# Three ordinary tiles instead of two ahead of the seven-product units, with the units' right factors prepared under the third

## The chip, the core and the metric

The kernel runs on one core of a Trainium2 chip. The metric is the device time of one execution in microseconds (us), as the median of several runs. The engines of the core are named PE (TensorE, matrix products), DVE (VectorE, elementwise), ACT (ScalarE, activations and casts), POOL (GpSimd) and SP (SyncE, which here only issues DMAs). Each of them takes its own instructions in order and waits on semaphores for the others.

## The reference

One layer of a residual block in float32, for 1024 positions of 1024 features:

```
def swiglu(h, w_gate, w_up, w_down):
    return (jax.nn.silu(h @ w_gate) * (h @ w_up)) @ w_down
...
x = x + 0.5 * swiglu(rmsnorm(x, ffn1_norm[l]), ffn1_w_gate[l], ffn1_w_up[l], ffn1_w_down[l])
x = x + hybrid_mixer(rmsnorm(x, mix_norm[l]), w_in[l], conv_w[l], conv_b[l], ...)
x = x + 0.5 * swiglu(rmsnorm(x, ffn2_norm[l]), ffn2_w_gate[l], ffn2_w_up[l], ffn2_w_down[l])
...
return rmsnorm(x, final_norm)
```

The two feed-forward parts (FFN1, FFN2) have 2816 hidden features, which is 22 tiles of 128. The mixer between them is a stick-breaking attention and a short convolution. The change touches only the first half of each feed-forward part, `silu(h @ w_gate) * (h @ w_up)`.

## The kernel before

Every float32 operand of a matrix product is split into a high and a low part: ACT casts the high part (`nc.scalar.copy`, line 169), DVE subtracts it from the operand (line 170). A product is then three matmuls (high by high, high by low, low by high). Activations lie with features on the 128 partitions and positions along the free axis, in two halves of 512 positions (`hf`). So `x` has 8 feature tiles by 2 halves.

`gate_up(i, act, started, nstd)` computes the 22 hidden tiles `m` of feed-forward part `i`. It does the first `nstd` of them (the table `STD`, line 433, gives 2 for each part) as **ordinary tiles**: for gate and then for up, 8 feature tiles by 2 halves by 3 matmuls, so 48 matmuls each and 96 for a tile. They need no normalised activations: `act` holds the split of `x` times the gain, and the factor 1/rms comes in later, on the products. `gated` (lines 449 to 451) scales the gate's product, takes its silu and scales it again; `hidden` (line 683) multiplies by the up product; `Aside.take` (line 649) forms sums and stores them to `c_sp` for the second half.

The remaining hidden tiles are **units**: gate and up weights of one tile are taken as a 2 by 2 block matrix and multiplied with the activations, also a 2 by 2 block matrix, by seven block products instead of eight (P1, P2, P7, P5, P6, Q4, P3). A product has 4 feature tiles of 3 matmuls, so a unit has 84 matmuls, and delivers the gate and the up of a tile. For this the activations must be combined and normalised, once for each part:

- `normed_in_place` (line 700) multiplies a tile of `x` by its gain and by 1/rms, 16 times;
- the generator `right` makes the right factors in the order P1, P2, P7, P5, P6, Q4, P3, 4 tiles each, as sums of normalised tiles (line 544) and their splits (lines 169 and 170). P1 needs four normalised tiles, P2 four others, P7 the eight of the second half.
- `left` makes the left factors of a unit from its weights, which lie in one buffer `raw`: a split for P2 and P1, three sums (lines 482 to 485), a split for P3 and P6, one for P7 and P5, one for Q4.

The first two units run together, product by product ("u.do(name)" for the one, then for the other), so that there are 24 matmuls for each right factor as it is made; all later units run alone. In FFN1 tile 0 is done during the start of the kernel, together with the transposes of `x`, and the call begins with tile 1.

A list scheduler orders each engine's instructions from the order of the program and its dependences; buffers come from pools (72 of 128 by 512 called `s`, 10 of 128 by 1024 called `w` for split weights, 2 of 128 by 2048 called `raw` for loaded weights, 8 PSUM banks `ps`). SP loads weights when a `raw` buffer is free.

Of the kernel before, what the change touches and what calls it, by code (L numbers as in the profile page):

```python
# [13 lines left out]
ALU = mybir.AluOpType  # L14
# [27 lines left out]
def hybrid_block(ctx: ExitStack, tc: tile.TileContext, t: dict):  # L42
    nc = tc.nc
    NK = D // P
# [9 lines left out]
    def nm(s):  # L54
        uid[0] += 1
        return f"{s}_{uid[0]}"

    def s(dt=F32):

        return sb.tile([P, HALF], dt, name=nm("s"), tag="s", bufs=72)  # L60

    def w4(dt=F32R):

        return sb.tile([P, S], dt, name=nm("w"), tag="w", bufs=10)

    def bank():
        return ps.tile([P, HALF], F32, name=nm("ps"), tag="ps", bufs=8)
# [22 lines left out]
    def mm(out, lhs, rhs, **kw):  # L90
        nc.tensor.matmul(out, lhs, rhs, **kw)  # L91
        clock[0] += 1
        while pending and pending[0][0] <= clock[0]:
            next_event()
# [73 lines left out]
    def split(hi, lo, x):  # L168
        nc.scalar.copy(hi, x)  # L169
        nc.vector.tensor_tensor(out=lo, in0=x, in1=f(hi), op=ALU.subtract)  # L170
        return hi, lo
# [47 lines left out]
    W = Stream()  # L219
# [9 lines left out]
    def wk(w, k):  # L229
        return (w[0][:, k * P : (k + 1) * P], w[1][:, k * P : (k + 1) * P])  # L230

    def both(outs, w, nk, rhs):

        for k in range(nk):
            first, last = k == 0, k == nk - 1
            wh, wl = wk(w, k)
            for hf in range(2):
                rh, rl = rhs(k, hf)
                mm(outs[hf], wh, rh, start=first, stop=False)
                yield  # L240
                mm(outs[hf], wh, rl, start=False, stop=False)
                yield
            for hf in range(2):
                mm(outs[hf], wl, rhs(k, hf)[0], start=False, stop=last)
                yield

    def run(gen):
        for _ in gen:
            pass
# [180 lines left out]


    VORDER = ((2, 6), (3, 7), (0, 4), (1, 5))
    STD = (2, 2)
    N_MIXER = 8 + 8 + 12 + 12

    def all_weights():
        yield from ffn_weights(0, "ffn1", STD[0])
        yield from mixer_weights()
        yield from ffn_weights(1, "ffn2", STD[1])

# [3 lines left out]
    def gated(g, act):  # L444

        o = [s(), s()]
        for hf in range(2):
            rms = act.row(hf)
            nc.vector.tensor_tensor(out=o[hf], in0=rms, in1=g[hf], op=ALU.mult)
            nc.scalar.activation(o[hf], o[hf], AF.Silu)  # L450
            nc.vector.tensor_tensor(out=o[hf], in0=o[hf], in1=rms, op=ALU.mult)
        return o
# [7 lines left out]
    def left(raw, n=HALF, late="P7"):  # L460


        a = {}

        def blk(i, m=1):
            return raw[:, i * n : (i + m) * n]

        def pair(dt=F32R):
            return w4(dt)[:, : 2 * n]

        def halves(hi, lo, *names):
            for i, name in enumerate(names):
                a[name] = (hi[:, i * n : (i + 1) * n], lo[:, i * n : (i + 1) * n])

        def two(ap):
            return ap.rearrange("p (n c) -> p n c", c=n)

        yield a
        halves(*split(pair(), pair(), blk(0, 2)), "P2", "P1")
        yield  # L480
        y = pair(F32)
        nc.vector.tensor_tensor(out=two(y), in0=two(blk(1, 2)), in1=blk(3).unsqueeze(1).to_broadcast([P, 2, n]),  # L482
                                op=ALU.add)
        nc.vector.tensor_tensor(out=blk(3), in0=y[:, :n], in1=blk(2), op=ALU.add)
        nc.vector.tensor_tensor(out=blk(0), in0=blk(3), in1=blk(0), op=ALU.add)
        yield

        def wide():
            hi, lo = pair(), pair()
            split(two(hi), two(lo), two(raw[:, : 4 * n])[:, 0::3])  # L490
            halves(hi, lo, "P3", "P6")

        def narrow():
            halves(*split(pair(), pair(), y), "P7", "P5")

        for step in (wide, narrow) if late == "P7" else (narrow, wide):
            step()
            yield
        a["Q4"] = split(s(F32R)[:, :n], s(F32R)[:, :n], blk(2))
        L.load()  # L500
        yield
# [33 lines left out]
    def right(x, y):  # L535

        b = {}
        yield b

        def parts(name, tiles):  # L540
            b[name] = [split(s(F32R), s(F32R), a) for a in tiles]

        def comb(out, i, j, op):
            nc.vector.tensor_tensor(out=out, in0=i, in1=j, op=op)  # L544
            return out

        def four(k0, hf):
            return [y(k0 + i, hf) for i in range(4)]

        b11 = four(4, 0)  # L550
        parts("P1", b11)
        yield
        b21 = four(0, 0)
        parts("P2", b21)
        yield
        b22, b12, t3 = [], [], []
        for i in range(4):
            b22.append(y(i, 1))
            b12.append(y(4 + i, 1))
            t3.append(comb(s(), b22[i], b12[i], ALU.subtract))  # L560
        parts("P7", t3)
        yield
        t1 = [comb(b11[i], b11[i], b12[i], ALU.subtract) for i in range(4)]
        parts("P5", t1)
        yield
        t2 = [comb(b12[i], t1[i], b22[i], ALU.add) for i in range(4)]
        parts("P6", t2)
        yield
        parts("Q4", [comb(b21[i], t2[i], b21[i], ALU.subtract) for i in range(4)])
        yield  # L570
        parts("P3", b22)
        yield
# [62 lines left out]
    class Aside:  # L635
# [12 lines left out]
        def comb(self, out, x, y, op):  # L648
            nc.vector.tensor_tensor(out=out, in0=x, in1=y, op=op)
            return out  # L650
# [26 lines left out]
    def gate_up(i, act, started, nstd):  # L677

        out = Aside(i)

        def hidden(m, o, u):
            for hf in range(2):
                nc.vector.scalar_tensor_tensor(out=o[hf], in0=o[hf], scalar=0.5, in1=u[hf], op0=ALU.mult,
                                               op1=ALU.mult)
                out.take(m, hf, o[hf])

        for m in range(nstd):
            if m == 0 and started:
                continue
            g, u = [bank(), bank()], [bank(), bank()]  # L690
            run(both(g, W(), NK, act))
            if m == 1 and started:
                hidden(0, gated(started[0], act), started[1])
            o = gated(g, act)
            run(both(u, W(), NK, act))
            hidden(m, o, u)

        def normed_in_place(k, hf):
            x = act.x[k, hf]
            nc.vector.scalar_tensor_tensor(out=x, in0=x, scalar=gain(act.gname, k), in1=act.row(hf),  # L700
                                           op0=ALU.mult, op1=ALU.mult)
            return x

        rights = right(act.x, normed_in_place)
        b = next(rights)
        preps = [left(L.take()[0]) for _ in range(2)]
        units = [Unit(next(p), b, out(nstd + j)) for j, p in enumerate(preps)]
        for p in preps:
            next(p)
        for name in ALL:  # L710
            next(rights)
            for p in preps:
                next(p, None)
            for u in units:
                u.do(name)
        act.x.clear()
        x_tiles.clear()
        prep = left(L.take()[0])
        a = next(prep)
        run(prep)  # L720
        for m in range(nstd + 2, NF):
            unit = Unit(a, b, out(m))
            if m + 1 < NF:
                prep = left(L.take()[0])
                a = next(prep)
            else:
                prep = iter(())
                makers[i] = Prep(i)
                makers[i].begin(0)
            for n, name in enumerate(FEW):  # L730
                unit.do(name)
                next(prep, None)
                if i in makers:
                    makers[i].step()
                    makers[i].upto(UPTO[0] * (n + 1))
            run(prep)
        makers[i].end()
# [234 lines left out]
    g, u = [bank(), bank()], [bank(), bank()]  # L972
# [4 lines left out]
    warm(2, turn(*turns.pop(0)))  # L977
    W.left = 2 * (STD[0] - 1)
    for k in range(NK):
# [14 lines left out]

    gate_up(0, act0, (g, u), STD[0])

# [19 lines left out]
    vt = []  # L1016
    W.left = N_MIXER + 2 * STD[1]
    for hf in range(2):
# [284 lines left out]
    for p in range(4):  # L1303
        for head, hf in ((2 * p, 0), (2 * p, 1), (2 * p + 1, 0), (2 * p + 1, 1)) if p < 3 else (
                (6, 0), (7, 0), (6, 1), (7, 1)):
            prev, y = None, []
            for b in range(4 * hf + 3, -1, -1):
                u, steps = unit(head, hf, b, prev, y)
# [39 lines left out]


    gate_up(1, act2, None, STD[1])  # L1350
    gb = [s(), s()]
    for i in range(2):
# [65 lines left out]
```

## Time and profile before

| | us |
|---|---|
| median of 3 runs | 1920.36 |
| lowest and highest of them | 1918.93, 1923.02 |
| the profiled execution, its own time | 1924.48 |
| its span, from the first to the last instruction | 1922.8 |
| PE busy in the span | 1835.9 (95%) |
| DVE busy | 1393.1 (72%) |
| ACT busy | 897.9 (47%) |

A row of a timeline gives the start, the time to the end of the last instruction, the engine, the line in the kernel, the operation, the tiles written and read, and how many instructions are merged into it; in brackets stands how long the engine was idle before it and which instruction of which engine ended that. Matmul rows go by the name of the helper's line (L91). Matmuls overlap: one of 512 columns has a mean duration of 394 ns in the profile, while back to back they follow each other more closely. A few per cent of the matmul records can be missing, so counts of matmuls are taken from the program.

### The profile page before, as it was taken

How to read it: one execution, taken by the hardware profiler on the slowest of the kernel's cores; microseconds unless marked ns; L12 is line 12 of the kernel's file. 1: busy time of each engine (PE TensorE's matmuls, PEld its weight loads, DVE VectorE, ACT ScalarE, POOL GpSimd, SP SyncE). 2: the span in 40 equal slices, each digit the busy share in tenths (PEclk: the TensorE clock that was granted, in tenths of full speed). 3: DMA queues.
4: the chain of work that ended last, by engine and by line, in shares of the span. 5: the costliest groups of instructions: out<-in, count | busy, mean ns of one | idle time of the engine just before them, and what ended most of it. 6: DMA issues, size and time to landing. Idle time of an engine off the chain costs nothing.

```text
span 1922.8 us, 23200 instructions
## 1 busy us (share of the span) xinstructions
PE 1835.9 (95%) x8176; PEld 1507.5 (78%) x8176; DVE 1393.1 (72%) x2179; ACT 897.9 (47%) x1608; POOL 253.5 (13%) x400
## 2 busy tenths in 40 slices
PE   6889999999999979999999999989999999988997
PEld 5668888888888858888888878867888888767775
DVE  4897667666777787668787898668676666755768
ACT  4543222223555554667677775533322222444544
POOL 1101001110222120110101000100010101021211
PEclk8899999999999999999999999989999999999998
DMA  7114323334999843341313343304333333588985
GB/s 236 65 55 131 110 90 108 112 104 143 239 230 230 229 165 83 80 99 34 94 44 72 100 142 111 106 33 122 105 108 113 101 102 108 169 184 200 207 195 176
DMA packets 252933, 246.93 MB, mean 128 GB/s; under 512 B 14176, under 2 KB 197008, under 8 KB 252816
## 3 DMA queue, kind: packets, MB, share of 16 engines
q1 hardware_dynamic: 217072, 157.87, 27.6%
q0 software_dynamic: 35744, 87.58, 18.0%
q8 instruction: 64, 1.05, 0.2%
q14 instruction: 53, 0.43, 0.1%
HBM read 150.76 MB, written 85.20 MB: 123 GB/s over the span
## 4 chain that ended last, share of the span: by engine, by line
PE 69%; issue 15%; DVE 9%; DMA 3%; POOL 3%; ACT 1%; SPq 1%; POOLq 0%; DVEq 0%; ACTq 0%
PE ps L91 68%; DVE w L170 1%; DVE s L870 1%; POOL r_sp L830 1%; DMA w<-c_sp 1%; POOL c_sp L646 1%; DVE s L170 1%; DMA raw<-in_ffn_w_gate 1%; DVE s L269 1%; DVE s L176 1%; PE ps L277 0%; DVE s L700 0%; DMA s<-x_sp 0%; PE ps L1087 0%; DVE s L544 0%
## 5 line engine op out<-in xcount | busy, mean ns | idle before, releaser
L91 PE MATMUL ps<-s,w 128*128 128x512 f32 x6352 | 1525.2, 394 | 61.7 <-ACT s L175 13.6
L91 PEld LDWEIGHTS ps<-s,w 128*128 128x128 f32 x6352 | 1192.3, 190 | 320.0 <-DVE s L170 17.4
L169 ACT CAST w<-raw 128x1024 fp32r<-128x1024 f32 (+2 forms) x158 | 157.5, 998 | 278.6 <-PE ps L91 187.9
L170 DVE TENSOR_TENSOR w<-raw,w 128x1024 fp32r<-128x1024 f32 (+2 forms) x158 | 182.0, 1153 | 117.6 <-PE ps L91 60.2
L91 PE MATMUL ps<-s,s 128*128 128x512 f32 (+3 forms) x968 | 249.0, 385 | 7.5 <-ACT s L853 6.5
L91 PEld LDWEIGHTS ps<-s,s 128*128 128x128 f32 x968 | 184.1, 191 | 48.9 <-ACT s L853 8.3
L646 POOL DMA_DIRECT2D c_sp<-s x154 | 83.5, 542 | 777.7 <-DVE s L632 610.9
L170 DVE TENSOR_TENSOR w<-w,w 128x768 fp32r<-128x768 f32 (+2 forms) x104 | 105.8, 1017 | 84.8 <-PE ps L91 44.3
L170 DVE TENSOR_TENSOR s<-s,s 128x512 fp32r<-128x512 f32 (+2 forms) x181 | 119.0, 670 | 43.1 <-ACT s L169 42.7
L169 ACT CAST w<-w 128x768 fp32r<-128x768 f32 (+2 forms) x104 | 91.7, 881 | 92.5 <-DMA w<-c_sp 41.6
L169 ACT CAST s<-s 128x512 fp32r<-128x512 f32 (+2 forms) x181 | 105.0, 607 | 51.6 <-DMA s<-c_sp 30.3
L628 ACT ACTIVATE s<-s 128x512 f32<-128x512 f32 x40 | 25.3, 633 | 201.6 <-DVE s L627 201.5
L170 DVE TENSOR_TENSOR s<-raw,s 128x512 fp32r<-128x512 f32 (+2 forms) x133 | 87.7, 667 | 24.2 <-ACT s L169 23.8
L169 ACT CAST s<-raw 128x512 fp32r<-128x512 f32 (+2 forms) x133 | 77.9, 602 | 36.4 <-DVE raw L766 36.4
L482 DVE TENSOR_TENSOR w<-raw 128x1024 f32<-128x1024 f32 (+2 forms) x56 | 63.1, 1128 | 43.4 <-PE ps L91 43.4
L613 ACT ACTIVATE s<-ps 128x512 f32<-128x512 f32 x40 | 23.8, 598 | 122.8 <-PE ps L91 122.8
L1241 DVE TENSOR_TENSOR s<-s,ps 128x128 f32<-128x128 f32 (+2 forms) x96 | 52.6, 548 | 16.8 <-ACT s L1237 16.4
L1229 ACT ACTIVATE s<-ps 128x128 f32<-128x128 f32 (+2 forms) x96 | 47.0, 490 | 37.7 <-PE ps L91 37.4
L619 DVE TENSOR_TENSOR s<-s,ps 128x512 f32<-128x512 f32 x40 | 27.4, 686 | 47.8 <-PE ps L91 47.8
L830 POOL DMA_DIRECT2D r_sp<-s x48 | 41.6, 876 | 154.7 <-DVE s L855 50.5
L1237 ACT ACTIVATE s<-s 128x128 f32<-128x128 f32 (+2 forms) x96 | 50.2, 523 | 20.6 <-DVE s L1233 19.3
L830 POOL DMA_DIRECT2D x_sp<-s x48 | 41.6, 866 | 125.4 <-DVE s L855 57.7
(133 smaller groups left out, 1697.2 us busy)
## 6 DMA issues: line engine op xcount, KB each, us to landing
c_sp<-s POOLq DMA_DIRECT2D x154, 256.0 KB, 2.5
raw<-in_ffn_w_gate SPq DMA_DIRECT2D x43, 512.0 KB, 3.9
raw<-in_ffn_w_up SPq DMA_DIRECT2D x43, 512.0 KB, 5.2
x_sp<-s POOLq DMA_DIRECT2D x80, 256.0 KB, 4.3
s<-c_sp SPq DMA_DIRECT2D x77, 256.0 KB, 6.5
r_sp<-s POOLq DMA_DIRECT2D x64, 256.0 KB, 5.1
w<-c_sp SPq DMA_DIRECT2D x72, 192.0 KB, 5.0
raw<-in_ffn_w_down SPq DMA_DIRECT2D x11, 1024.0 KB, 8.9
```

What stands on the lines that cost most here:

```text
L91: nc.tensor.matmul(out, lhs, rhs, **kw)
L169: nc.scalar.copy(hi, x)
L170: nc.vector.tensor_tensor(out=lo, in0=x, in1=f(hi), op=ALU.subtract)
L482: nc.vector.tensor_tensor(out=two(y), in0=two(blk(1, 2)), in1=blk(3).unsqueeze(1).to_broadcast([P, 2, n]), op=ALU.add)
L613: last_silu[0] = nc.scalar.activation(self.s0, o, AF.Silu)
L619: nc.vector.tensor_tensor(out=self.u3, in0=self.u2, in1=self.o[2], op=ALU.add)
L628: last_silu[0] = nc.scalar.activation(self.u2, self.u2, AF.Silu)
L646: nc.gpsimd.dma_start(out=self.sp[FACTORS.index(self.names[i]), j], in_=x)
L830: nc.gpsimd.dma_start(out=self.acc(self.g + 4 * i, hf), in_=x, accum_op=ALU.add)
L1229: behind(nc.scalar.activation(u["s"][:, cols], u["z"][:, cols], AF.Exp), table_set)
L1237: nc.scalar.activation(sc, sc, AF.Ln, bias=1.0)
L1241: nc.vector.tensor_tensor(out=sc, in0=sc, in1=u["z"][:, cols], op=ALU.max)
```

## The change

`STD` becomes 3 for both parts. The right factors' generator is started before the loop over ordinary tiles. Under the last ordinary tile it is advanced by one step between the gate's and the up's products (P1's four normalisations and splits) and by two after `hidden` (P2's; then the normalisation of the other eight tiles, for which `right` gets a step of its own). The loop over products skips the steps that were made. Each part so has 3 ordinary tiles and 19 units, of which the pair is tiles 3 and 4.

```
-    STD = (2, 2)
+    STD = (3, 3)
...
-        b22, b12, t3 = [], [], []
-        for i in range(4):
-            b22.append(y(i, 1))
-            b12.append(y(4 + i, 1))
-            t3.append(comb(s(), b22[i], b12[i], ALU.subtract))
+        b22, b12 = four(0, 1), four(4, 1)
+        yield
+        t3 = [comb(s(), b22[i], b12[i], ALU.subtract) for i in range(4)]
         parts("P7", t3)
...
+        rights = right(act.x, normed_in_place)
+        b = next(rights)
         for m in range(nstd):
             if m == 0 and started:
                 continue
+            ahead = m == nstd - 1
             g, u = [bank(), bank()], [bank(), bank()]
             run(both(g, W(), NK, act))
             if m == 1 and started:
                 hidden(0, gated(started[0], act), started[1])
             o = gated(g, act)
+            if ahead:
+                next(rights)
             run(both(u, W(), NK, act))
             hidden(m, o, u)
-
-        def normed_in_place(k, hf):
...
-        rights = right(act.x, normed_in_place)
-        b = next(rights)
+            if ahead:
+                next(rights)
+                next(rights)
+
         preps = [left(L.take()[0]) for _ in range(2)]
...
         for name in ALL:
-            next(rights)
+            if name not in b:
+                next(rights)
```

PE has 8058 instructions before and 8082 after. How the queues read at the places in question follows, for FFN1; FFN2 reads alike. In the changed file line 683 is 681, 700 is 687 and 649 is 647.

The first place is DVE's queue where the ordinary tiles end and the units begin. Before, from `hidden` of tile 1 (L683, which reads the up product `ps`) to the first low parts of P1's right factors (L170, `s<-s,s`) and of the units' weights (L170, `w<-raw,w`); between them stand normalisations (L700) and the sums of `Aside` (L649):

```order
L683 SCALAR_TENSOR_TENSOR s_638<-s_638,ps_501 128x512
L683 SCALAR_TENSOR_TENSOR s_639<-s_639,ps_502 128x512
L700 SCALAR_TENSOR_TENSOR s_195<-s_195,gains_146,s_570 128x512
L649 TENSOR_TENSOR s_698<-s_635,s_639 128x512
L649 TENSOR_TENSOR s_623<-s_639,s_623 128x512
L649 TENSOR_TENSOR s_703<-s_698,s_638 128x512
L700 SCALAR_TENSOR_TENSOR s_215<-s_215,gains_146,s_570 128x512
L170 TENSOR_TENSOR s_719<-s_235,s_718 128x512
L170 TENSOR_TENSOR w_793<-raw_492,w_792 128x1024
L170 TENSOR_TENSOR s_723<-s_253,s_722 128x512
```

After, the same place in the program, P1's low parts and `hidden` of tile 2 (L681); L451 is the last step of `gated` of tile 2, L485 a sum of weights, L544 the sums for P5:

```order
L170 TENSOR_TENSOR s_787<-s_253,s_786 128x512
L485 TENSOR_TENSOR raw_654<-raw_654 128x512
L170 TENSOR_TENSOR s_791<-s_271,s_790 128x512
L485 TENSOR_TENSOR raw_725<-raw_725 128x512
L170 TENSOR_TENSOR s_795<-s_289,s_794 128x512
L170 TENSOR_TENSOR w_927<-raw_654,w_926 128x1024
L544 TENSOR_TENSOR s_235<-s_235,s_378 128x512
L544 TENSOR_TENSOR s_253<-s_253,s_393 128x512
L544 TENSOR_TENSOR s_271<-s_271,s_411 128x512
L544 TENSOR_TENSOR s_289<-s_289,s_426 128x512
L681 SCALAR_TENSOR_TENSOR s_770<-s_770,ps_713 128x512
L681 SCALAR_TENSOR_TENSOR s_771<-s_771,ps_714 128x512
```

All of P1's low parts now stand ahead of `hidden` of the last ordinary tile, where before they stood behind it.

The second place is DVE's queue from P2's right factors to P7's. Before, with P5's sums first (three of L544), then the low part of the first unit's P7 and P5 weights (L170, `w<-w,w`), the four differences for P7 (L544), the same weights of the second unit, and P7's first low part:

```order
L544 TENSOR_TENSOR s_235<-s_235,s_378 128x512
L544 TENSOR_TENSOR s_253<-s_253,s_393 128x512
L544 TENSOR_TENSOR s_271<-s_271,s_411 128x512
L170 TENSOR_TENSOR w_861<-w_734,w_860 128x1024
L544 TENSOR_TENSOR s_830<-s_307,s_378 128x512
L544 TENSOR_TENSOR s_834<-s_325,s_393 128x512
L544 TENSOR_TENSOR s_838<-s_345,s_411 128x512
L544 TENSOR_TENSOR s_842<-s_360,s_426 128x512
L170 TENSOR_TENSOR w_865<-w_738,w_864 128x1024
L170 TENSOR_TENSOR s_845<-s_830,s_844 128x512
```

After, with P2's four low parts first (L170, `s<-s,s`):

```order
L170 TENSOR_TENSOR s_857<-s_159,s_856 128x512
L170 TENSOR_TENSOR s_861<-s_175,s_860 128x512
L170 TENSOR_TENSOR s_865<-s_195,s_864 128x512
L170 TENSOR_TENSOR s_869<-s_215,s_868 128x512
L170 TENSOR_TENSOR w_987<-w_888,w_986 128x1024
L544 TENSOR_TENSOR s_962<-s_307,s_378 128x512
L544 TENSOR_TENSOR s_964<-s_325,s_393 128x512
L544 TENSOR_TENSOR s_966<-s_345,s_411 128x512
L544 TENSOR_TENSOR s_968<-s_360,s_426 128x512
L170 TENSOR_TENSOR w_991<-w_892,w_990 128x1024
L170 TENSOR_TENSOR s_971<-s_962,s_970 128x512
```

P2's low parts have come together ahead of it and no normalisation stands there any more; the order from the first unit's weights over the four differences to P7's first low part is the same.

The third place is PE at the end of P2. Before, the matmuls of the two units (banks `ps_742` and `ps_757`) alternate to the end, and P7 (`ps_868`) begins:

```order
L91 MATMUL ps_757<-s_785,w_710 128x512
L91 MATMUL ps_757<-s_784,w_711 128x512
L91 MATMUL ps_742<-s_789,w_706 128x512
L91 MATMUL ps_742<-s_788,w_707 128x512
L91 MATMUL ps_757<-s_788,w_710 128x512
L91 MATMUL ps_757<-s_789,w_710 128x512
L91 MATMUL ps_757<-s_788,w_711 128x512
L91 MATMUL ps_868<-s_844,w_860 128x512
```

After, the first unit's P2 (`ps_896`) is finished before the second's (`ps_911`) begins, as it stands in FFN2 before the change too:

```order
L91 MATMUL ps_896<-s_868,w_880 128x512
L91 MATMUL ps_896<-s_869,w_880 128x512
L91 MATMUL ps_896<-s_868,w_881 128x512
L91 MATMUL ps_911<-s_856,w_884 128x512
L91 MATMUL ps_911<-s_857,w_884 128x512
L91 MATMUL ps_911<-s_856,w_885 128x512
```

Between the two programs nothing else is in another order on PE, ACT or DVE than these stretches of FFN1 and FFN2; POOL's and SP's queues hold the same kinds of instructions in the same order.

## Rows read from the trace of the kernel before

**Rows 1.** The page: the span, and busy time of the engines.
```profile
span 1922.8 us, 23200 instructions
...
PE 1835.9 (95%) x8176; PEld 1507.5 (78%) x8176; DVE 1393.1 (72%) x2179; ACT 897.9 (47%) x1608; POOL 253.5 (13%) x400
```

**Rows 2.** The page: shares by engine of the chain that ended last.
```profile
PE 69%; issue 15%; DVE 9%; DMA 3%; POOL 3%; ACT 1%; SPq 1%; POOLq 0%; DVEq 0%; ACTq 0%
```

**Rows 3.** Timeline of PE in FFN1, from 60 to 140 us.
```profile
74.01 12.18 PE L91 MATMUL ps<-s,w 128*128 128x512 f32 x53
91.43 6.78 PE L91 MATMUL ps<-s,w 128*128 128x512 f32 x22 [5.24 <-DVE s L170]
99.49 6.06 PE L91 MATMUL ps<-s,w 128*128 128x512 f32 x24 [1.28 <-ACT s L169]
108.27 1.22 PE L91 MATMUL ps<-s,w 128*128 128x512 f32 x2 [2.72 <-ACT s L169]
111.17 20.71 PE L91 MATMUL ps<-s,w 128*128 128x512 f32 x82 [1.67 <-DVE s L170]
131.71 5.60 PE L91 MATMUL ps<-s,s 128*128 128x512 f32 x24
```

**Rows 4.** Timeline of PE in FFN2, from 1232 to 1400 us.
```profile
1233.44 34.65 PE L91 MATMUL ps<-s,w 128*128 128x512 f32 x152
1269.30 0.51 PE L91 MATMUL ps<-s,w 128*128 128x512 f32 x1 [1.20 <-ACT s L169]
1272.78 6.81 PE L91 MATMUL ps<-s,w 128*128 128x512 f32 x23 [2.98 <-DVE s L170]
1280.83 6.00 PE L91 MATMUL ps<-s,w 128*128 128x512 f32 x24 [1.24 <-ACT s L169]
1288.60 0.73 PE L91 MATMUL ps<-s,w 128*128 128x512 f32 x2 [1.76 <-ACT s L169]
1290.66 21.42 PE L91 MATMUL ps<-s,w 128*128 128x512 f32 x82 [1.33 <-DVE s L170]
1311.92 0.39 PE L91 MATMUL ps<-s,s 128*128 128x512 f32 x1
...
1354.57 2.88 PE L91 MATMUL ps<-s,s 128*128 128x512 f32 x12
...
1373.61 2.88 PE L91 MATMUL ps<-s,s 128*128 128x512 f32 x12
```

**Rows 5.** Timeline of DVE, FFN1, as the ordinary tiles end.
```profile
86.37 1.27 DVE L683 SCALAR_TENSOR_TENSOR s<-s,ps 128x512 f32<-128x512 f32 x2
...
88.23 1.88 DVE L649 TENSOR_TENSOR s<-s,s 128x512 f32<-128x512 f32 x3
...
90.03 0.74 DVE L700 SCALAR_TENSOR_TENSOR s<-s,gains,s 128x512 f32<-128x512 f32 x1
90.70 0.68 DVE L170 TENSOR_TENSOR s<-s,s 128x512 fp32r<-128x512 f32 x1
```

**Rows 6.** Busy time of DVE under ordinary tiles: stretch, length, PE, PEld, DVE, ...
```profile
60.00:86.00 26.00, 26.00 (x111) 21.27 (x110) 21.09 (x37) 14.14 (x29) 4.14 (x4) 0.93 0.06 21
1234.00:1268.00 34.00, 34.00 (x151) 27.88 (x149) 23.50 (x35) 6.22 (x9) 1.08 (x2) 1.00 0.05 17
```

**Rows 7.** Timeline of DVE in FFN2 at P7.
```profile
1285.24 1.22 DVE L170 TENSOR_TENSOR w<-w,w 128x1024 fp32r<-128x1024 f32 x1 [1.93 <-ACT w L169]
1286.38 2.49 DVE L544 TENSOR_TENSOR s<-s,s 128x512 f32<-128x512 f32 x4
1288.79 1.22 DVE L170 TENSOR_TENSOR w<-w,w 128x1024 fp32r<-128x1024 f32 x1
```

**Rows 8.** Stretches after P7's waits: length, PE busy, granted clock (1.00 is 2.4 GHz).
```profile
108.00:116.00 8.00, 6.06 (x15) 0.57 0.00 0
1289.00:1297.00 8.00, 6.67 (x19) 0.57 0.00 0
```

**Rows 9.** The page: weight loads, KB each, median us from issue to landing.
```profile
raw<-in_ffn_w_up SPq DMA_DIRECT2D x43, 512.0 KB, 5.2
```

More of the change, by code (lines that the diff above doesn't have):

```diff
@@ L685, in hidden @@
                 out.take(m, hf, o[hf])
[L687 to L696, printed above, removed]
         def normed_in_place(k, hf):
@@ L705, in gate_up @@
         b = next(rights)
+        for m in range(nstd):
+            if m == 0 and started:
+                continue
+            ahead = m == nstd - 1
+            g, u = [bank(), bank()], [bank(), bank()]
+            run(both(g, W(), NK, act))
+            if m == 1 and started:
+                hidden(0, gated(started[0], act), started[1])
+            o = gated(g, act)
+            if ahead:
+                next(rights)
+            run(both(u, W(), NK, act))
+            hidden(m, o, u)
+            if ahead:
+                next(rights)
+                next(rights)
         preps = [left(L.take()[0]) for _ in range(2)]
```

## The prediction

> **What bounds the kernel now.** I read the page first: PE is busy 95% of a span of 1922.8 us, DVE 72% [rows 1], and of the chain that ended last 69% lies on PE, 15% is issue and only 9% is DVE [rows 2]. So PE's own instructions bound the kernel, and what can be had besides is found where PE stands still. The change works at one place in each feed-forward part, so next I read PE's timeline there. What the reader is to see is the bracket at the start of each row. In FFN1 PE waits 5.24 us for a low part before P1, 1.28 us before P2, 2.72 and 1.67 us in P7 [rows 3]; in FFN2 1.20 and 2.98 us, 1.24 us, 1.76 and 1.33 us [rows 4]. Then DVE's timeline at the same place: from 86.37 us it does `hidden` (L683), the sums (L649) and the last normalisation (L700), and only at 90.70 us the first low part of P1 [rows 5]. PE waits for a queue of DVE, not for data that are missing.
>
> **The price of a matmul.** A steady unit has 84 matmuls and comes round from 1354.57 to 1373.61 us [rows 4], so 19.04 us, or 0.2267 us a matmul. As the profile gives one 0.39 us (the single matmul at 1311.92 us [rows 4]), a run of matmuls ends in its row 0.17 us after the next could have started. I take that off wherever a run ends.
>
> **What P1 and P2 lose now.** P1 and P2 of the pair have 24 matmuls each, which should take 5.44 us.
> - FFN1 [rows 3]: tile 1 ends at 74.01 + 12.18 - 0.17 = 86.02. P1 starts at 91.43, a loss of 5.41. It ends at 91.43 + 6.78 - 0.17 = 98.04, after 6.61 us, 1.17 too many. P2 starts at 99.49, 1.45 later, and ends at 105.38, 0.45 too late. Together 8.48 us.
> - FFN2 [rows 4]: tile 1 ends at 1267.92, P1 at 1272.78 + 6.81 - 0.17 = 1279.42. That is 11.50 us for 5.44, a loss of 6.06. P2 starts at 1280.83 (1.41) and ends at 1286.66 (0.39). Together 7.86 us.
>
> These 16.34 us are what the change can remove by its own aim. They include what the clock cost after the first wait, since they are counted by time and not by the brackets.
>
> **What P7 loses now.** From the end of P2 to the first matmul of Q4 there are 84 matmuls (P7, P5, P6 of the pair, P1 of the next unit), 19.04 us. FFN1 takes 131.71 - 105.38 = 26.33, a loss of 7.29 us [rows 3]; FFN2 1311.92 - 1286.66 = 25.26, a loss of 6.22 us [rows 4]. Of the 6.22 us, 3.09 are the two waits. The rest is the clock: over the 8 us after P7 begins its mean is 0.57 [rows 8], so with levels of 0.5 and 1 it was at the lower one for 0.43 / 0.5 x 8 = 6.9 us.
>
> **What is added.** An ordinary tile has 96 matmuls and replaces a unit of 84. Twice 12 matmuls are the 24 by which PE's queue grows: 24 x 0.2267 = +5.44 us. Nothing hides them, since PE is what is waited for. The units' product work on DVE and ACT gets less by a unit in each part; neither is the bound there, so I count nothing for it. Loads stay equal in number and bytes. The third tile's two matrices go into two `raw` buffers in place of one; the next two loads then wait for these to be split. They land 5.2 us after their issue [rows 9], and a tile lasts 96 x 0.2267 = 21.76 us, so this is hidden, by about a tile.
>
> **What is moved, and whether it fits.** DVE has room under the ordinary tiles: it is busy 21.09 of 26 us in FFN1 and 23.50 of 34 us in FFN2 [rows 6], and the third tile gives another 21.76 us. Steps on DVE from the rows: 0.60 us for an operation of 512 columns (three in 1.88 us), 0.67 for a normalisation (90.03 to 90.70) [rows 5], 1.14 for one of 1024 columns (1285.24 to 1286.38) [rows 7].
>
> FFN1, along the changed queue from 86.37 us, where `hidden` of tile 1 can start, to P1's last low part: 3 normalisations (2.0), 4 operations of 1024 columns on the units' weights (4.6), and 17 of 512 columns (2 of `hidden`, 3 of `Aside`, 4 of `gated`, 4 sums of weights, 4 low parts: 10.2). The sum is 16.8 us, so 103.2 us. PE ends tile 2 at 86.02 + 21.76 = 107.78: P1's factors are there 4.6 us early. In FFN2 the queue waits for tile 2's gate product, at 1267.92 + 10.88 = 1278.80, and has about 7.3 us to go from there, so 1286.1 against 1289.68. P1 starts without a wait in both.
>
> P2's low parts stand behind `hidden` of tile 2. From its start these are 2 x 0.60, one of 1.14, one sum of 0.60 and 4 x 0.60, so 5.3 us, while PE spends 5.44 us on P1. As P2 uses its four tiles one after the other, 0.68 us each, the last is needed 2 us later. So both losses go, 16.34 us.
>
> **Where the stall goes: P7 stays.** Its four differences (L544) stand behind the low part of the first unit's P7 weights (L170, `w<-w,w`) in DVE's queue, before and after. DVE is held at that row until ACT has cast these weights (the bracket of 1.93 us) and then does it at 1285.24, the differences at 1286.38, the second unit's weights at 1288.79 [rows 7], and P7's first low part behind them; PE waits for a cast of the differences and then for that low part. The chain starts from the end of the first unit's P2, and the change does not move it ahead of that. So I let P7 lose in both parts what FFN2 loses now, 6.22 us. For FFN1 that is a gain of 7.29 - 6.22 = 1.07 us, since there the two units' P2 now run one after the other as in FFN2, and the first unit's ends a good 2 us sooner.
>
> **The sum.** -16.34 + 5.44 - 1.07 = -11.97 us. The profiled execution took 1924.48 us, 4.12 above the median of 1920.36. 1924.48 - 11.97 = 1912.5, on the scale of the median 1908.4.
>
> **Bounds of the uncertain terms.** What P7 costs is bounded below by its two waits alone (3.09 us) and above by FFN1's 7.29 us: -3.1 to +1.1 us for each part. What remains of P1's and P2's losses is 0 by the queue's count, and at most all of it.
>
> **The rivals.**
> - *The clock is not cut at P7.* For it: before, P7's waits of 1.76 and 1.33 us come some 15 us after a longer stop [rows 4], and the waits of 1.28 and 1.24 us before P2 are followed by matmuls at full rate (24 in 6.06 and 6.00 us). With P1's stop gone, PE comes to P7 from an unbroken run. Against it: P7's own two waits with two matmuls between are unchanged, and the clock fell right behind them in both parts [rows 8]. It saves 3.1 us in each part: 1905.3 or 1902.2 us. The Trainium skill (TensorE: Matmul & The Clock Gate, Part 1) says that the gate follows how busy PE has been of late, and that idling brings the lower rate back. Taken for the whole stretch, that rule gives this rival's time; taken for P7's own waits alone, it gives the forecast. The rows do not decide between the two.
> - *A part of the wait returns.* DVE's count has 4.6 and 3.6 us of slack before P1. But ACT casts the second unit's weights ahead of P1's four tiles, and both engines wait for `w` buffers that PE frees; a wait of 3 us in one or both parts, now before P1 or P2, gives 1911 to 1915 us.
> - *It works in one part only*, for instance because FFN2's queue, which stands at tile 1's `hidden` until 1267.9 us, runs later than counted: 7.9 us come back, 1916.3 us.
> - *Slower: the pair's weights come late.* The second unit's `raw` buffer is now the one that tile 2's up matrix occupies until it is split, where before all four matrices of the pair were asked for long ahead. ACT holds all P1 casts behind the cast of this buffer. P1 then starts when the load lands, and DVE's rows behind it shift along. Against it: the split stands under tile 1, more than 20 us ahead, against 5.2 us for a load [rows 9]. It decides once P1 starts over 6 us after tile 2's end in both parts: then the 12 us are eaten and the time is 1920 or more; with all of P1's and P2's losses still there it is 1920.4 + 5.4 = 1925.8 us. That is also the time if the change does not do what it says.
>
> **How the numbers follow.** Forecast 55%; no cut of the clock in one part or both 22%; a part of the wait 13%; one part only 5%; slower or no change by late weights 5%. The range of 1902 to 1916 us holds the first three. Forecast alone: 1906 to 1911. A difference of 0.2% (3.8 us) is about what a measurement of this kernel can tell from none. The first three lie beyond that, and the one-part case by a hair, so I count half of it as no change: faster 0.90, same 0.06, slower 0.04.
>
> **What would show it.** In the changed profile PE should run without a wait of half a us from 60 us to the end of P2 in FFN1, at 86.02 + 21.76 + 10.88 = 118.7 us. FFN1 gains 8.48 + 1.07 - 2.72 = 6.83 us, so P2 of FFN2 should end at 1267.92 - 6.83 + 32.64 = 1293.7 us, again with nothing before it. Two short waits should follow each, released by ACT L169 and DVE L170, and the clock's mean behind them should be near 0.57 (forecast) or near 1 (first rival). PE has 24 matmuls more. A wait before P1 released by ACT or by a load would show the second or the last rival. The forecast is wrong if the new queue stalls where I counted it as free, above all at `w` buffers, which I counted from the order alone, or if other stretches of the kernel change with no cause in the program's order.

## The result, and the profile after

| | before | after | ratio, 95% interval |
|---|---|---|---|
| medians, us (4 and 4 runs) | 1921.44 | 1905.76 | 0.9912 [0.9894, 0.9930] |
| profiled execution: its time, its span | 1924.48, 1922.8 | 1899.17, 1897.4 | |

The kernel is faster by 15.7 us. The execution that was profiled after is the fastest of its four (the others took 1904.0 to 1909.4), and that of before was above its median, so 25.4 us lie between the two traces. Page of after, which answers to [rows 1]:

```profile
span 1897.4 us, 23215 instructions
PE 1828.5 (96%) x8200; PEld 1504.0 (79%) x8200; DVE 1381.8 (73%) x2167; ACT 892.7 (47%) x1602; POOL 252.8 (13%) x400
```

PE does 24 matmuls more (8200 for 8176) in less busy time. PE's timeline of after, FFN1 [rows 3]; the last row begins Q4 of tile 12:

```profile
72.47 44.39 PE L91 MATMUL ps<-s,w 128*128 128x512 f32 x195
118.40 0.73 PE L91 MATMUL ps<-s,w 128*128 128x512 f32 x2 [1.54 <-ACT s L169]
120.46 20.39 PE L91 MATMUL ps<-s,w 128*128 128x512 f32 x82 [1.33 <-DVE s L170]
140.69 0.39 PE L91 MATMUL ps<-s,s 128*128 128x512 f32 x1
141.68 5.89 PE L91 MATMUL ps<-s,s 128*128 128x512 f32 x23 [0.60 <-DVE s L617]
...
297.25 2.88 PE L91 MATMUL ps<-s,s 128*128 128x512 f32 x12
```

The same of FFN2 [rows 4]; the last row is Q4 of tile 6, which before begins at 1373.61:

```profile
1224.94 67.29 PE L91 MATMUL ps<-s,w 128*128 128x512 f32 x296
1293.83 0.73 PE L91 MATMUL ps<-s,w 128*128 128x512 f32 x2 [1.59 <-ACT s L169]
1295.89 19.03 PE L91 MATMUL ps<-s,w 128*128 128x512 f32 x82 [1.33 <-DVE s L170]
1314.76 0.39 PE L91 MATMUL ps<-s,s 128*128 128x512 f32 x1
...
1357.14 2.88 PE L91 MATMUL ps<-s,s 128*128 128x512 f32 x12
```

The reader is to see the first row of each: 195 and 296 matmuls in one run, to the end of P2, without a bracket. The brackets of 5.24 and 1.28 us [rows 3], 1.20, 2.98 and 1.24 us [rows 4] are gone; P7's two are still there, and FFN1 has a new one of 0.60 us in the pair's Q4. The 195 also tell what the rows of before hold. Up to the end of P2 the change adds the 96 matmuls of one tile, and 195 - 96 = 99 are the 53 + 22 + 24 of [rows 3]. P1 has 24, so its first two stand in the row of 53, ahead of the wait, and 51 are tile 1's.

**How much of it lies at the changed places.** In each part I measure from the first matmul behind the sums of squares (74.01 and 1233.44 before, 72.47 and 1224.94 after) to Q4 of a tile that both programs do as a unit. Tile 12 of FFN1 before, on PE's timeline:

```profile
306.95 2.88 PE L91 MATMUL ps<-s,s 128*128 128x512 f32 x12
```

FFN1 takes 232.94 us before and 224.78 after, FFN2 (to tile 6) 140.17 and 132.20: -8.2 and -8.0, together -16.1 us. That is about the gain of the medians. The other 9 us of the profiles lie behind tile 6 of FFN2 (-8.9 us; 1.5 us less ahead of FFN1 and 1.2 us more between the parts nearly cancel), almost all in the last 270 us, where the programs are alike. The windows over that stretch, to the end of the span (stretch, length, busy time of PE, PEld, DVE, ACT, POOL, the granted clock, and last the DMA's share and GB/s), of before, of after, and of two more executions of the changed kernel (experiments *again* and *again2*):

```profile
1660.00:1930.00 270.00, 230.31 (x947) 183.63 (x946) 180.60 (x293) 121.46 (x222) 51.51 (x61) 0.94 0.77 192
```
```profile
1643.00:1930.00 287.00, 225.18 (x948) 179.32 (x947) 180.96 (x294) 121.91 (x223) 51.39 (x61) 0.97 0.72 180
```
```profile
1647.00:1930.00 283.00, 226.38 (x945) 180.34 (x943) 179.89 (x292) 122.31 (x222) 51.43 (x61) 0.96 0.73 183
```
```profile
1648.00:1930.00 282.00, 231.17 (x948) 182.84 (x947) 181.04 (x294) 122.25 (x223) 51.37 (x61) 0.94 0.74 183
```

The same matmuls keep PE busy for 225.2, 226.4 and 231.2 us in one and the same program, with the clock at a mean of 0.97, 0.96 and 0.94; before, with 230.3 us, lies among them. The windows reach past the end of the span; up to it they are 262.8, 254.4, 257.2 and 262.7 us long. One and the same program takes up to 8 us more here in one execution than in another, so these 9 us are no sign of the change.

### The profile page after: what moved, and what is told of

It reads as the page before. It is cut to its first block, busy times and chain, and to the rows that moved or that the text cites. A ratio compares the mean times of both kernels' runs of the same rounds, so it can differ in the third digit from the quotient of the medians.

```text
span 1897.4 us, 23215 instructions
## 1 busy us (share of the span) xinstructions
PE 1828.5 (96%) x8200; PEld 1504.0 (79%) x8200; DVE 1381.8 (73%) x2167; ACT 892.7 (47%) x1602; POOL 252.8 (13%) x400
## 4 chain that ended last, share of the span: by engine, by line
PE 55%; issue 28%; DVE 7%; POOL 4%; DMA 3%; ACT 1%; SPq 1%; POOLq 0%; DVEq 0%; ACTq 0%
PE ps L91 54%; POOL c_sp L644 2%; DVE s L875 1%; DMA w<-c_sp 1%; POOL r_sp L835 1%; DVE w L170 1%; DVE s L269 1%; DVE s L176 1%; DVE s L170 1%; DMA s<-c_sp 1%; DMA raw<-in_ffn_w_gate 0%; DMA raw<-in_ffn_w_down 0%; ACT w L169 0%; DMA s<-in_x 0%; PE ps L277 0%
## 5 line engine op out<-in xcount | busy, mean ns | idle before, releaser
L91 PE MATMUL ps<-s,w 128*128 128x512 f32 (+1 forms) x6400 | 1523.1, 392 | 40.9 <-DVE s L845 13.3
L170 DVE TENSOR_TENSOR w<-raw,w 128x1024 fp32r<-128x1024 f32 (+2 forms) x158 | 181.8, 1153 | 111.3 <-PE ps L91 55.6
L91 PE MATMUL ps<-s,s 128*128 128x512 f32 (+3 forms) x944 | 242.7, 383 | 8.4 <-ACT s L858 6.0
L91 PEld LDWEIGHTS ps<-s,s 128*128 128x128 f32 x944 | 178.7, 190 | 49.0 <-ACT s L858 7.9
L170 DVE TENSOR_TENSOR w<-w,w 128x768 fp32r<-128x768 f32 (+2 forms) x102 | 103.3, 1013 | 77.8 <-PE ps L91 40.6
L170 DVE TENSOR_TENSOR s<-s,s 128x512 fp32r<-128x512 f32 (+2 forms) x181 | 118.7, 670 | 40.8 <-ACT s L169 40.3
L170 DVE TENSOR_TENSOR s<-raw,s 128x512 fp32r<-128x512 f32 (+2 forms) x131 | 86.2, 666 | 24.0 <-ACT s L169 23.6
L611 ACT ACTIVATE s<-ps 128x512 f32<-128x512 f32 x38 | 22.7, 598 | 113.2 <-PE ps L91 113.2
```

The lines of the kernel that those rows point to most:

```text
L611: last_silu[0] = nc.scalar.activation(self.s0, o, AF.Silu)
```

## The experiments

Each version is timed against the kernel before on its chip, in five rounds. The columns FFN1 and FFN2 give the difference to before of the two stretches just defined, from each version's one trace, matched matmul by matmul (for *four* some units later); the median is that of all runs.

| version | FFN1 | FFN2 | sum | median | ratio, 95% interval |
|---|---|---|---|---|---|
| again | -8.3 | -7.9 | -16.1 | -16.2 | 0.9915 [0.9899, 0.9931] |
| again2 | -8.2 | -5.4 | -13.6 | -14.9 | 0.9916 [0.9896, 0.9936] |
| tile_only | -1.9 | +1.7 | -0.2 | -1.3 | 0.9998 [0.9981, 1.0014] |
| move_only | +1.1 | -10.4 | -9.2 | -8.5 | 0.9959 [0.9945, 0.9973] |
| four | -5.8 | -4.8 | -10.6 | -8.9 | 0.9958 [0.9944, 0.9973] |
| p1_late | -4.2 | -1.9 | -6.1 | -8.1 | 0.9960 [0.9947, 0.9972] |
| p2_late | -7.3 | -5.8 | -13.1 | -14.9 | 0.9930 [0.9911, 0.9949] |
| two_three | +2.5 | -6.7 | -4.2 | -7.1 | 0.9960 [0.9945, 0.9975] |
| three_two | -8.2 | -8.0 | -16.2 | -18.7 | 0.9899 [0.9878, 0.9921] |
| t3early | -7.5 | -5.9 | -13.4 | -13.8 | 0.9918 [0.9894, 0.9942] |
| lead | -12.0 | -10.5 | -22.5 | -19.8 | 0.9896 [0.9878, 0.9915] |
| lead_three_two | -12.0 | -14.0 | -26.0 | -25.2 | 0.9866 [0.9847, 0.9885] |

The theory: P1 and P2 waited for DVE's and ACT's queues, and the gain comes from the factors' low parts standing ahead of the last tile's finish, with a tile to hide under. The main rival: the third tile does it alone, since the scheduler brings normalisations forward by itself.

**again, again2** (the changed kernel). 

> The changed kernel once more, nothing altered. If the gain lies where the trace shows it, the P1 and P2 waits are gone again in both parts, the ratio to before is 0.991 to 0.994 (about -12 to -16 us), and the step from P7 to the next product differs between the two parts only with the granted clock there. If part of the 15.7 us came from a lucky clock in the last stage, the time comes out nearer -12 us and the last stage shows about the cuts of before.

> The changed kernel unaltered, on the chip of the next three, so that they are compared with it directly. Theory: 0.991 to 0.993 of before, as in its two earlier comparisons (0.9912 and 0.9915), with no wait ahead of P1 and P2, and at P7 the same two waits; whether a cut of the granted clock follows them differs from one execution to the next.

Both held: P1 and P2 have no wait in either, and the ratio came out alike three times. They also show how one program differs from execution to execution at P7. In *again2* the second part loses 2.6 us more there, with the same brackets (1.59 and 1.33 us). Windows of the 10 us from P7's start, FFN1 and FFN2, of the first trace of after, then of *again2*:

```profile
118.00:128.00 10.00, 8.28 (x29) 6.41 (x29) 10.00 (x17) 7.21 (x14) 0.00 (x0) 0.83 0.01 2
1294.00:1304.00 10.00, 8.67 (x37) 6.80 (x38) 10.00 (x17) 6.64 (x13) 0.00 (x0) 1.00 0.00 0
```
```profile
121.00:131.00 10.00, 8.17 (x28) 6.36 (x29) 10.00 (x17) 7.31 (x14) 0.00 (x0) 0.83 0.01 2
1296.00:1306.00 10.00, 8.46 (x23) 6.40 (x24) 10.00 (x17) 7.01 (x14) 0.00 (x0) 0.66 0.00 0
```

FFN2's clock there is 1.00 in one and 0.66 in the other; no other difference shows at that place.

**tile_only** (the kernel before with the third tile).

```
-    STD = (2, 2)
+    STD = (3, 3)
```

> The kernel before with three ordinary tiles per part, the factor code left where it was. Theory (the factors' low parts must stand ahead of the last tile's finish on VectorE): that finish still stands in front of P1's factors, so a wait of 3.5 to 4 us stays ahead of P1 in each part and the third tile costs 5.4 us: -2 to -6 us against before, ratio 0.997 to 0.999. Rival 1 (the third tile alone gives the cover, since the normalisations slip under it by themselves): the same as the changed kernel, -12 us or more, ratio 0.991 to 0.993. Rival 2 (a tile without moved code only adds products): +5 us, ratio 1.003.

The main rival fell: without the moved code the gain is gone (0.9998). The theory had the place right and the size too favourable (it said -2 to -6 us). PE's timeline of FFN2:

```profile
1233.79 56.41 PE L91 MATMUL ps<-s,w 128*128 128x512 f32 x248
1291.45 0.73 PE L91 MATMUL ps<-s,w 128*128 128x512 f32 x2 [1.25 <-ACT s L169]
1293.69 8.17 PE L91 MATMUL ps<-s,w 128*128 128x512 f32 x22 [1.50 <-DVE s L170]
1303.06 5.99 PE L91 MATMUL ps<-s,w 128*128 128x512 f32 x24 [1.19 <-ACT s L169]
```

The brackets ahead of P1 and P2 add up to 3.94 us, against 5.42 before [rows 4]. But behind them 22 matmuls take 8.17 us, so P1 and P2 lose 7.97 us here (1303.06 + 5.99 - 0.17, less the tile's end at 1290.03 and 10.88), as much as the 7.86 of before: the clock's mean in the 10 us from 1291 is 0.66. In FFN1, with the same three waits but the clock at 1.00, P1 and P2 lose 5.1 us, against 8.9 before: there the third tile hides something, and costs 2.72 us. Why P1 waits is seen on DVE, here FFN1:

```profile
107.12 1.28 DVE L683 SCALAR_TENSOR_TENSOR s<-s,ps 128x512 f32<-128x512 f32 x2 [5.35 <-PE ps L91]
108.33 1.22 DVE L170 TENSOR_TENSOR w<-raw,w 128x1024 fp32r<-128x1024 f32 x1
109.46 0.68 DVE L649 TENSOR_TENSOR s<-s,s 128x512 f32<-128x512 f32 x1
110.06 1.29 DVE L170 TENSOR_TENSOR s<-s,s 128x512 fp32r<-128x512 f32 x2
```

DVE stands idle for 5.35 us at `hidden` of the last tile (L683), which needs PE's last product, and P1's first low part (110.06) stands behind it. ACT's queue is in the same case, and PE's first wait ahead of P1 (1.25 us) is for it. ACT, FFN1 of *tile_only*, then of after:

```profile
106.94 1.05 ACT L169 CAST w<-raw 128x1024 fp32r<-128x1024 f32 x1 [7.50 <-PE ps L91]
107.89 2.18 ACT L169 CAST s<-s 128x512 fp32r<-128x512 f32 x4
```
```profile
97.29 1.65 ACT L169 CAST s<-s 128x512 fp32r<-128x512 f32 x3
```

In *tile_only* P1's four casts (107.89) stand behind a cast of the units' weights that PE releases only as the tile ends; in after the last three of them are made at 97.29, far ahead of P1 (105.81). There is time enough; it is the order that costs, on both engines. No run changes the order on one of them alone, so what each is worth is not shown.

**p1_late, p2_late** (one half of the move undone in each).

p1_late:

```
             o = gated(g, act)
-            if ahead:
-                next(rights)
             run(both(u, W(), NK, act))
             hidden(m, o, u)
             if ahead:
+                next(rights)
                 next(rights)
                 next(rights)
```

p2_late:

```
         b22, b12 = four(0, 1), four(4, 1)
-        yield
...
             hidden(m, o, u)
-            if ahead:
-                next(rights)
-                next(rights)
```
 

> The changed kernel with one line moved: P1's factors are made behind the last ordinary tile's finish instead of ahead of it; P2's and the other normalisations stay where they are, ahead of the units' weights. Theory (the finish, which waits for the tile's last product, then stands on VectorE in front of P1's four low parts): P1 waits again for ScalarE and VectorE in turn, 1.3 and 1.5 us as with the third tile alone, in both parts, with up to two cuts of the clock: +5 to +10 us against the changed kernel, ratio to before 0.994 to 0.997. Rival (only P2's place matters, or the scheduler brings the factors forward by itself): the same as the changed kernel within 2 us.

> The changed kernel with the other half undone: P1's factors under the last tile's up as changed, P2's factors and the last four pairs of normalisations back in the units' loop. Theory (the gain splits by the waits): P1 starts without a wait, P2 waits again for ScalarE by about 1.2 us per part behind the units' weights, as with the third tile alone: +2.5 to +6 us against the changed kernel, ratio to before 0.9925 to 0.995. Rival (once P1 is early, P2's factors are ready in time wherever they stand in the code): the same as the changed kernel within 1.5 us.

P1's place is worth some 7 us (0.9960 against 0.9916 on the same chip): the waits of 1.25 and 1.51 us are back ahead of P1 in both parts, and nothing is left ahead of P2. P2's place is worth too little to be told by the medians (both 1907.7 us; the intervals of the ratios overlap), so the 2.5 to 6 us of the theory are not shown. Its wait is back in the trace of *p2_late* in both parts, PE in FFN2:

```profile
1231.24 61.85 PE L91 MATMUL ps<-s,w 128*128 128x512 f32 x272
1294.28 6.00 PE L91 MATMUL ps<-s,w 128*128 128x512 f32 x24 [1.19 <-ACT s L169]
```

**move_only, three_two, two_three, four** (the changed kernel with (2, 2), (3, 2), (2, 3) and (4, 4) in the table `STD`). 

> The changed kernel with two ordinary tiles per part, so the factors are still made under and after the last of them, and the third tile's 5.44 us aren't paid. Theory (VectorE has too much to do under one tile in the first part, which starts with a tile less to hide under): the first part keeps a wait of 4 to 6 us at P1 of the second unit, the second part keeps under 2 us: -8 to -13 us against before, ratio 0.993 to 0.996, so the third tile is worth only 0 to 4 us by itself. Rival 1 (the move does it all, the third tile only costs): -17 us or more, ratio 0.991 or less, faster than the changed kernel. Rival 2 (without the third tile nothing is hidden): within 3 us of before.

> The changed kernel with three ordinary tiles in the first part and two in the second (factors still ahead of the units in both). Matched product by product, the runs so far put the first part at -7.9 us with three tiles and +1.3 with two, the second at -8.0 with three and -10.3 with two (the clean walk from tile to unit, without the third tile's 2.7 us). Theory (the parts add, and only the first needs the third tile): -18 us against before, ratio 0.990 to 0.991, some 2 us faster than the changed kernel. Rival (the second part's result with two tiles was a lucky clock): the same as the changed kernel or slower, ratio 0.992 or more.

> The other way round: two ordinary tiles in the first part, three in the second. Theory (the parts add): +1.3 and -8.0, -6.7 us against before, ratio 0.996 to 0.997, slower than every other version with the factors ahead. Rival (the first part's long wait with two tiles was an accident of one execution): -12 us or more, ratio 0.994 or less.

> The changed kernel with four ordinary tiles per part. Theory (all that there was to hide is hidden under the third, and each tile more replaces 84 products by 96, at 0.227 us each, 2.72 us per part): 5.4 us slower than the changed kernel, ratio to before 0.994 to 0.997. Rival (the tile hides something more, such as the wait at P7): no slower than the changed kernel.

The move without the third tile gives half of the gain, and all of that in FFN2 (-10.4 us). In FFN1 PE waits 7.39 us in P1, more than I expected. *move_only*, PE, and below it DVE with L687 the normalisations:

```profile
72.03 15.18 PE L91 MATMUL ps<-s,w 128*128 128x512 f32 x65
94.59 10.43 PE L91 MATMUL ps<-s,w 128*128 128x512 f32 x34 [7.39 <-DVE w L170]
```
```profile
92.05 0.75 DVE L687 SCALAR_TENSOR_TENSOR s<-s,gains,s 128x512 f32<-128x512 f32 x1
92.71 0.69 DVE L170 TENSOR_TENSOR s<-s,s 128x512 fp32r<-128x512 f32 x1
93.31 1.23 DVE L170 TENSOR_TENSOR w<-raw,w 128x1024 fp32r<-128x1024 f32 x1
```

P1's right factors are in time there; the second unit's weights (93.31) are late, behind the normalisations and low parts for P2. With two tiles FFN1 has 51 matmuls of ordinary tiles left behind its row sums [rows 3], FFN2 152 [rows 4]. *two_three* has the same bracket in FFN1 (7.38) and came out at 0.9960, as said. *three_two* came out at 0.9899, as said too if the parts add. In its one trace FFN2 gains no more than with three tiles (-8.0 us): of the tile saved, measured against *move_only*, 1.6 us went to a cut of the clock at P7 (0.83 over 10 us) and 0.8 us to waits behind it. Its interval overlaps that of the changed kernel, so that it is faster is not shown. *four* is slower than the changed kernel, by 5.5 us in the traces' parts and 7.2 us in the medians: the fourth tile hides nothing that shows and costs its 24 matmuls.

**lead, t3early** (P7's wait). `lead` makes each right factor one product earlier; `t3early` moves only the four differences of P7 ahead, into the step before.

lead:

```
         for name in ALL:
-            if name not in b:
-                next(rights)
+            if name != "P1":
+                next(rights, None)
```

t3early:

```
         b22, b12 = four(0, 1), four(4, 1)
-        yield
         t3 = [comb(s(), b22[i], b12[i], ALU.subtract) for i in range(4)]
+        yield
         parts("P7", t3)
```

> The changed kernel with each right factor made one step earlier than now, so that P7's four differences and their casts stand on VectorE and ScalarE ahead of the units' P7 weights. Theory (at P7 the matmuls wait for two short chains in turn, the weights' cast on ScalarE and the low parts on VectorE, because the factor is made only then; no transfer is late): both waits (1.54 and 1.33 us per part) shrink to under 0.5 us together, the wait of 0.6 us at P4 too, and no cut of the granted clock follows: -5 to -9 us against the changed kernel, ratio to before 0.986 to 0.989. Rival 1 (the waits are for the weights, which the factor's work ahead only delays): the first wait grows by what the second loses, within 2 us of the changed kernel. Rival 2 (the work moved ahead makes P2 late): slower than the changed kernel by 2 us or more.

> The changed kernel with only P7's four differences moved ahead on VectorE, ScalarE's order as it is. Theory: the wait of 1.33 us for VectorE's low parts goes, the one of 1.54 us for ScalarE's casts stays, and whether the clock is cut after it tells if two waits or one bring the cut: -2.5 us against the changed kernel if the cut stays, -4 if it goes, ratio to before 0.989 to 0.991. Rival (ScalarE's cast of the factor comes last anyway): the second wait turns into one for ScalarE, the same time as the changed kernel.

In the trace of *lead* P7's waits are gone. PE in FFN2:

```profile
1224.08 83.97 PE L91 MATMUL ps<-s,w 128*128 128x512 f32 x368
1308.42 0.50 PE L91 MATMUL ps<-s,w 128*128 128x512 f32 x1 [0.37 <-ACT w L169]
```

One run of 368 matmuls now goes through P7. From P2's end to Q4, PE loses 1.1 and 1.0 us in the two parts. The clock stays at 1.00 behind P7 in both. A new wait of 1.2 to 1.4 us, for a low part of weights, comes 38 matmuls behind the pair's Q4. What had been late is seen on ACT in the trace of after, FFN1:

```profile
113.95 1.05 ACT L169 CAST w<-w 128x1024 fp32r<-128x1024 f32 x1 [1.91 <-PE ps L91]
114.90 0.59 ACT L611 ACTIVATE s<-ps 128x512 f32<-128x512 f32 x1
116.30 1.05 ACT L169 CAST w<-w 128x1024 fp32r<-128x1024 f32 x1 [0.80 <-DVE w L170]
117.25 0.59 ACT L611 ACTIVATE s<-ps 128x512 f32<-128x512 f32 x1
117.74 4.25 ACT L169 CAST s<-s 128x512 fp32r<-128x512 f32 x8
```

The casts of P7's differences (117.74) stand behind the casts of both units' weights and behind what empties the banks of P2 (L611), while PE has ended P2 at 116.69. In *lead*, where P2 ends near 119.5, the first of these casts comes at 114.80, ahead of the weights':

```profile
114.80 0.62 ACT L169 CAST s<-s 128x512 fp32r<-128x512 f32 x1
116.81 1.06 ACT L169 CAST w<-w 128x1024 fp32r<-128x1024 f32 x1 [1.39 <-PE ps L91]
```

By the parts `lead` gains 6.4 us on *again*, as expected; by the medians of two chips some 3.6 us (0.9896 and 0.9915), less than expected, and the intervals overlap, so the medians alone do not show it to be faster.

`t3early` did what neither theory said. The scheduler put eleven of the sums and differences (L544) ahead of the first unit's P7 weights. Its DVE, FFN1:

```profile
111.81 6.70 DVE L544 TENSOR_TENSOR s<-s,s 128x512 f32<-128x512 f32 x11
118.43 1.21 DVE L170 TENSOR_TENSOR w<-w,w 128x1024 fp32r<-128x1024 f32 x1
```

The low part of these weights comes 1.1 us behind the end of P2 (117.36), where in after it comes 1.7 us ahead of it; P7's waits grew to 1.97 and 1.81 us, and P7 loses 7.0 and 7.1 us, with the clock at 0.66 over 10 us in both parts. So it says nothing about one wait against two; it only suggests that these weights belong to the chain too, and why the first wait, which is for ACT, grew is not shown.

**lead_three_two** (the edit of `lead`, and (3, 2) in the table).

> Each right factor one step earlier, and three ordinary tiles in the first part, two in the second. Theory (what the third tile hides in the second part is little, and with P7's waits gone no cut of the clock there eats the 2.7 us): -11.7 us in the first part as with the earlier factors alone, -10.5-2.7 = -13.2 in the second: ratio to before 0.987 to 0.989, 2 to 3 us faster than the earlier factors with three tiles in both (0.9896), and 5 to 9 us faster than the changed kernel. Rival (with one tile less of cover the factors made still earlier come late in the second part): a wait of 1 us or more ahead of P1 or P2 there, no faster than the earlier factors with three tiles.

It came out at 0.9866, 10.3 us faster than the changed kernel on the same chip (1897.39 and 1907.72 us), and their intervals do not overlap; 5 to 9 us were said. A wait came back in FFN2, as the rival has it, though two matmuls into P7 and for weights. PE:

```profile
1270.29 16.16 PE L91 MATMUL ps<-s,w 128*128 128x512 f32 x70 [1.12 <-DVE w L170]
```

It is one short wait, and no cut of the clock follows. By the parts FFN2 gains 3.5 us on *lead*, so the tile that is saved is worth more than the wait; by the ratios, from two chips, the intervals of the two overlap.

## Why the prediction was right, and where it was off

The forecast was 1908.4 us, within 1902 to 1916, and a gain of 11.97 us; 1905.8 and 15.7 us were measured. Two steps of it are large and one small.

- **P1 and P2: held.** They were to lose nothing. After, 195 matmuls end at 72.47 + 44.39 - 0.17 = 116.69, so in 44.22 us, and at 0.2267 us each they need 44.21; in FFN2 296 take 67.12 us and need 67.10. So all of the loss is gone. It was 16.79 us, though, and not 16.34: the prediction put the end of FFN1's tile 1 behind 53 matmuls, at 86.02, and it is behind 51, at 85.57, so P1 and P2 lost 8.93 us there and not 8.48. The queue count held as well. On DVE in after, FFN1:

```profile
100.85 0.68 DVE L170 TENSOR_TENSOR s<-s,s 128x512 fp32r<-128x512 f32 x1
...
105.79 1.28 DVE L681 SCALAR_TENSOR_TENSOR s<-s,ps 128x512 f32<-128x512 f32 x2 [0.71 <-PE ps L91]
...
108.73 2.49 DVE L170 TENSOR_TENSOR s<-s,s 128x512 fp32r<-128x512 f32 x4
```

  P1's last low part is done near 101.5 and P1 begins at 116.69 - 10.88 = 105.81: 4.3 us early, where 4.6 was said. From `hidden` to P2's last low part it is 5.4 us, where 5.3 was said. That this order is the cause is shown by *tile_only* and *p1_late*. The prediction counted DVE's queue; ACT's, which *tile_only* shows to hold P1 too, it named only as a risk.
- **The 24 matmuls: held.** +5.44 us was said, and after the change 195 and 296 matmuls go at this price without a gap. *four*, which adds 24 again, costs 5.5 us by its parts, but so exactly only by chance: the clock is not cut at FFN1's P7 there (1.4 us less), and more is lost behind P7 (1.6 us).
- **P7: mis-sized.** The step was "So I let P7 lose in both parts what FFN2 loses now, 6.22 us", a gain of 1.07 us. It lost 140.69 - 116.69 - 19.04 = 4.96 us in FFN1 and 1314.76 - 1292.06 - 19.04 = 3.66 us in FFN2, so it gained 2.33 + 2.56 = 4.89 us. In FFN1 the brackets shrank from 4.39 to 2.87 us, for which the prediction had allowed, and the rest of the loss from 2.90 to 2.09. In FFN2 the brackets stayed (3.09 and 2.92) and the rest fell from 3.13 to 0.74, with the clock at 1.00. So not all of that rest was the clock, as the prediction took it: with equal brackets the cut costs 2.7 us (6.37 us lost in FFN2 of *again2*, 3.66 in after), where the prediction priced it at 3.1. The 6.37 us are the size that the forecast let P7 have. With the terms as measured the sum is -16.79 + 5.44 - 4.89 = -16.2 us, and behind P7 FFN1 loses 0.4 us and FFN2 gains 0.3: -16.1, as in the traces, against -15.7 in the medians.
- **The rivals.** My forecast assumed the clock cut behind P7 in both parts. The first rival, no cut in one part, gave 1905.3 us, and that is nearer to the 1905.8 measured than the forecast is; that it comes so near is partly luck, since FFN1's P7 gained as well and the cut was priced too high. In the trace of after and in *again* FFN2 has no cut and FFN1 a short one; in *again2* both have one. The prediction set two readings of the Trainium skill (TensorE: Matmul & The Clock Gate, Part 1) against each other, PE's whole recent stretch or P7's waits alone; the same program behaves in both ways, so no single reading gives the time. No wait returned at P1 or P2, no part was left out, and the pair's weights were not late. In *move_only*, however, the weights did come late on DVE, in FFN1; there the third tile is the cover that the prediction named.

The prediction let P7's chain start from the end of the first unit's P2; that was only the order of this program. *lead* shows that it can be broken.

## What to carry to other kernels

When a matrix engine waits for operands that an elementwise engine makes, look first at what stands ahead of them in the queue of every engine that makes them. Here a finish step on DVE and a cast of weights on ACT, which both waited for PE, stood ahead of parts that could have been ready long before. In FFN2 moving them was enough (-10.4 us without the third tile, +1.7 with the tile alone). In FFN1 neither did much by itself (+1.1 and -1.9 us), and both together gave -8.2. Ask of each stretch by itself how much cover it needs, since the tile that paid in FFN1 was not needed in FFN2.

## What I had not expected of the hardware

P7's two short waits, 1.54 to 1.60 and 1.32 or 1.33 us with two matmuls between and an unbroken run of matmuls before them, stand in twelve stretches of these traces (two each in after, *again*, *again2*, *three_two* and *four*, one each in *two_three* and *move_only*). In seven of them the granted clock fell to its lower level (1.2 GHz) for a while (means of 0.83 or 0.66 over 10 us), in five it stayed at 1.00. P7 lost 3.5 to 3.7 us without a cut, 4.9 to 5.1 with a mean of 0.83, and 6.4 with one of 0.66. What decides is open: the brackets do not differ, and in *p2_late*, with longer ones (1.77 and 1.81, then 1.33 us, and 1.19 us before P2), the clock stayed at 1.00 in both parts. With these two waits gone (*lead*, *lead_three_two*) there was no cut in any of four stretches.
